# Opening of a one-core trunk kernel: key weights by a second queue, later loads behind the memory's splits, x's tiles later among the weight folds

## The chip, the cores and the metric

The kernel runs on one core of a Trainium2 chip. The time is that of the whole program on that core, in microseconds of the device, measured from outside; a profiled execution gives in addition a trace of every instruction. PE is the matmul engine, DVE the vector engine, ACT the scalar (activation) engine, POOL the general one, SP the engine that mostly issues DMAs. ACT can issue DMAs too, on a queue of its own. Each engine runs its instructions in the order in which they stand in its own stream, and waits for others by semaphores.

## The reference

A decoder layer of width 1024 over 2048 tokens: retention and a pooling mixer, then cross-attention into 256 memory tokens, then a gated MLP with a short convolution, each behind an RMSNorm and with a residual. Only this part matters here:

```python
def cross_attn(h, mem_n, wq, wkv, wo):
    q = (h @ wq).reshape(B, S, XA_HEADS, XA_HEAD_DIM)
    k, v = jnp.split(mem_n @ wkv, 2, axis=-1)
    ...
    s = jnp.einsum('bshd,bmhd->bhsm', q, k).astype(jnp.float32) * (XA_HEAD_DIM ** -0.5)
    p = jax.nn.softmax(s, axis=-1).astype(v.dtype)
    o = jnp.einsum('bhsm,bmhd->bshd', p, v).reshape(B, S, D_MODEL)
    return o @ wo
```

`mem_n` is the memory behind its RMSNorm. Keys and values depend on the memory and the weights alone, so the kernel folds `wq` into the keys and `wo` into the values once, ahead of the tokens. The layer's first step on the tokens, `rmsnorm(x, mix_norm_g)`, is also begun in that time.

## The kernel before

**Numbers.** Every float32 operand of a matmul is split into a high and a low part (`split`, L260 on): ACT writes the high part, DVE the low part (the source minus the high part), and `passes` (L276 to L278) makes three matmuls of each product: high by high, high by low, low by high. A weight tile of 128 x 1024 (512 KB) thus needs a load, one ACT and one DVE instruction before PE can use it.

**The opening** is `folded_weights` (from L428), a generator that a loop at L2087 runs item by item. The items, by number, are: keys K0 to K7 (items 0 to 7), values V0 and V1 (8, 9), then score folds M, values V, output folds O and pool folds W mixed:

```
0-7 K0..K7   8 V0   9 V1   10 M0   11 V2   12 M1   13 V3   14 M2   15 V4   16 M3
17 O0   18 V5   19 O1   20 V6   21 O2   22 V7   23 W0   24 W1   25 O3   26 W2   27 W3
```

- K*n* (`keys`, `project`) multiplies weight tile `wkv[n]` with the memory: 8 x 3 matmuls of 128 x 256. I write w0 to w15 for the tiles `wkv[0]` to `wkv[15]`; w8 to w15 are those of the values V0 to V7 (`memory_values`). With K2 the memory's norm is begun (`memory_norm`, L488): two squares on ACT, sums on DVE, and small matmuls (L357) with a column of the constants. With K7 the norm is spread over the keys (`spread`, L382) and the keys are scaled by it on DVE and split (`scaled_keys`, `parted`).
- M*h* (`score_weights`) needs the scaled and split keys of head *h* and two tiles of `wqT`: 48 matmuls of 128 x 256. Its results go to DRAM (`Md`) by ACT's queue.
- O*h* (`output_weights`) needs the values and two tiles of `wo`; W (`pool_weights`) one tile of `wout_p`.

**Places.** Loaded tiles stand in nine raw places of 512 KB: R0 to R2, S0, S1, Z0 to Z3 (L2084). A list gives out the place that was given back first. A weight's place is given back at once in program order (`new_raw`), so the next load into it waits only for the two splits of the tile before. An x tile (`load_x_wide`, L648) takes a place, is loaded by SP, split into `X` by ACT and DVE, squared in place by ACT and added to a running total by DVE; only then can its place be loaded again. The total stands in R0. The split parts of a weight stand in five wide places, used in turn.

In the order of before the list gives: w0 S0, w1 S1, w2 to w5 Z0 to Z3, w6 S0, w7 S1, x1 Z0, w8 R1, x2 R2, w9 Z1, x3 Z2, then M0's two tiles Z3 and S0, V2's weights S1, x4 Z0, M1's two tiles R1 and R2. R1 and R2 hold the memory at first.

**Order.** A planner orders each engine's stream by times of its own: among the instructions that it takes to be ready it places the one that stands first in the program, so that a load whose place is free can be moved ahead of loads that wait. `tc.keep_in_program_order` ties an instruction behind the one traced just before it on the same engine, and no more; `tc.issue_after` ties a block's instructions behind a named one. All four steps on an x tile, its load, and the splits of the memory and of w0 are tied in this way.

**Loads at the start.** L451 loads the memory in four parts of 256 KB, L453 the two halves of w0 (256 KB each) between them, L454 w1, all on SP; ACT issues the load of `vecs` (112 KB). L525 loads the constants (335.5 KB) with K1. Other sizes: `poolT` 256 KB and the positions twice 128 KB, whose calls stand with M3 and behind the folds. ACT's first work is its table load and one small activation (L455), then the splits in this order: memory 0, w0's first half, memory 1 to 3, w0's second half, memory 4 to 7. PE runs 9 small matmuls on a constant tile meanwhile (L458).

The x tiles come behind the items that L2086 names: x0 behind item 5, x1 behind 7, x2 behind 8, x3 behind 9, x4 behind 11, x5 behind 13, x6 behind 16, x7 behind 18. Behind item 21 the total goes through small matmuls (`rows_norm`, L2008), whose result is needed when the first values of the retention are evicted.

Of the kernel before, what the change touches and what calls it, by code (L numbers as in the profile page):

```python
# [22 lines left out]
SUB = 512  # L23
# [119 lines left out]
def trunk(ctx, tc, xT, memT, pos, w_qkgu, w_v, wkv, wqT, wo, wout_r, wout_p, poolT, w_up, w_dn, vecs, consts, outT):  # L143
# [136 lines left out]
    def new_raw():  # L280
        r = raws.take()
        r.free()
        return r.f
# [61 lines left out]
    def load_tile(src, room=None):  # L345
        raw = new_raw() if room is None else room.f
        fetched[0] = sp.dma_start(raw, src.rearrange("p k n -> p (k n)"))
        return raw
# [82 lines left out]
    def folded_weights():  # L431
# [17 lines left out]
        for q in range(4):  # L449
            to = memory[q // 2].f[:, q % 2 * SUB : (q % 2 + 1) * SUB].rearrange("p (k m) -> p k m", m=NMEM)  # L450
            sp.dma_start(to, memT.rearrange("(k p) m -> p k m", p=P)[:, 2 * q : 2 * q + 2])  # L451
            if q < 2:
                sp.dma_start(first[:, q * SUB : (q + 1) * SUB], wkv[0][:, 4 * q : 4 * q + 4].rearrange("p k n -> p (k n)"))  # L453
        second = load_tile(wkv[1])  # L454
        tc.keep_in_program_order(act.activation(warm.f[:, P : 2 * P], warm.f[:, :P], AF.Identity))  # L455
        lead = mmps()
        for _ in range(9):
# [8 lines left out]
        def wide_pair(raw, parts=1):  # L466
            u, w = wide(), T // parts
            for i in range(parts):
                split(raw[:, i * w : (i + 1) * w], *(r[:, i * w : (i + 1) * w] for r in u))
            return u  # L470
# [6 lines left out]
        u0 = wide()  # L477
        for k in range(KT):
            h, j = divmod(k, 4)
            split(memory[h].f[:, j * NMEM : (j + 1) * NMEM], mh[:, k], ml[:, k], memg[:, k : k + 1], kept="both")  # L480
            if k in (0, 3):
                at = slice(k // 3 * SUB, (k // 3 + 1) * SUB)
                split(first[:, at], u0[0][:, at], u0[1][:, at], kept="both")
        rm = TT.take()
        rn = smp.tile([P, 4], F32, tag="rnm", name="rnm", bufs=1)[:, :2]
        bank, done = [], []
# [11 lines left out]

        def project(n):

            u = u0 if n == 0 else wide_pair(second, 2) if n == 1 else wide_pair(load_tile(wkv[n]))
            if n % 2 == 0:
                bank[:] = [mmps()]
            at = n % 2 * NMEM
            ps = bank[0][:, at : at + NMEM]
            for k in range(KT):
                passes(ps, [r[:, k * P : (k + 1) * P] for r in u], (mh[:, k], ml[:, k]), k == 0, k == KT - 1)
# [13 lines left out]
        def keys(n):  # L521

            project(n)
            if n == 1:
                sp.dma_start(cs_t, consts)  # L525
            elif n == 2:
                memory_norm()
            if n % 2:
                done.append((n, bank[0]))
            if n == KT - 1:  # L530
                spread(rn, [rm.f[:, :NMEM]], late=True, behind=latest[0].ins)
                for pair in done:
                    scaled_keys(*pair)
                rm.free()
# [1548 lines left out]
    under[0], spacing[0] = weight_sums(), 2  # L2083
    raws = Places([(R, j * T) for j in range(3)] + [(r, 0) for r in S] + [(Z.arenas[0].t, j * T) for j in range(4)], T)  # L2084
    results = Places([(Z.arenas[1].t, j * T) for j in range(4)], T)
    wv, total, x_at = [], raws.take(), (5, 7, 8, 9, 11, 13, 16, 18)  # L2086
    for n, _ in enumerate(folded_weights()):  # L2087
        if n in x_at:
            load_x_wide(x_at.index(n), total)
        if n == 21:  # L2090
            total.back = None
            rn = rows_norm([total])
        if n in (24, 25):
            wv.append(value_weights(len(wv), 0))
        if n == 27:
            wv += [value_weights(kp, kp - 1) for kp in (2, 3)]
# [354 lines left out]
```

## Time and profile before

| | us |
|---|---|
| median of 3 runs | 2389.47 (2388.07 to 2391.1) |
| the profiled execution's own time | 2389.53 |
| its span in the trace | 2387.8 |
| PE busy | 2368.7 |
| DVE busy | 1796.6 |
| ACT busy | 1385.8 |
| POOL busy | 337.9 |

The span runs from the first to the last instruction of the trace; the time outside it is start and end of the launch. "Busy" is the time in which an engine runs at least one instruction. PE's matmuls overlap in the trace, so a busy PE can still run at a lower clock; the granted clock stands beside the busy times where stretches are listed. In a row of a timeline, "idle before" in square brackets is the time for which the engine stood still ahead of the instruction, with what ended it. The time to landing of a DMA runs from its issue to the semaphore that tells its end. The opening takes the first 116 us or so.

### The profile page before, as it was taken

What the parts mean: (1) busy time and instruction counts of PE and PEld (TensorE: products, weight loads), DVE (VectorE), ACT (ScalarE), POOL (GpSimd) and SP (SyncE); (2) the same over time, 40 slices, a digit from 0 to 9 for tenths busy, and PEclk for the clock granted to TensorE, in tenths of its full rate; (3) what the DMA queues carried; (4) which work ended last, traced back from release to release, by engine and by line L of the source; (5) the groups of instructions that cost most, each with busy time, mean ns of one, the idle gap of its engine ahead of it and who ended that gap; (6) DMA issues with size and microseconds to landing.
All of it is one profiled execution on the core that took longest, in us unless ns stands there. A gap on an engine that the chain in (4) does not pass through costs nothing.

```text
span 2387.8 us, 33436 instructions
## 1 busy us (share of the span) xinstructions
PE 2368.7 (99%) x11136; PEld 1980.8 (83%) x11136; DVE 1796.6 (75%) x2977; ACT 1385.8 (58%) x2507; POOL 337.9 (14%) x524
## 2 busy tenths in 40 slices
PE   8999999999999999999999999999999999999998
PEld 8888888888888888888888888888888888888886
DVE  8687876885767677866788776977677698877876
ACT  7845554663545545545655555855555577676663
POOL 0056554453041000000000010110000000000000
PEclk9999999999999999999999999999999999999999
DMA  8999999999594235486577564765455489768951
GB/s 308 343 285 294 280 264 285 284 308 310 164 260 123 79 119 159 151 281 228 170 238 251 179 199 135 243 207 176 150 177 188 136 261 316 234 183 284 343 174 73
DMA packets 269453, 527.78 MB, mean 221 GB/s; under 512 B 30048, under 2 KB 50912, under 8 KB 269280
## 3 DMA queue, kind: packets, MB, share of 16 engines
q1 hardware_dynamic: 212176, 402.83, 51.5%
q0 software_dynamic: 40960, 94.40, 16.5%
q10 hardware_dynamic: 16144, 28.43, 3.2%
q8 instruction: 87, 1.43, 0.2%
q14 instruction: 86, 0.70, 0.1%
HBM read 423.30 MB, written 196.61 MB: 260 GB/s over the span
## 4 chain that ended last, share of the span: by engine, by line
PE 97%; DMA 1%; DVE 1%; ACT 0%; issue 0%; SPq 0%; DVEq 0%; ACTq 0%
PE mm L276 30%; PE mm L278 30%; PE mm L277 30%; PE aux L276 1%; PE aux L278 1%; PE aux L277 1%; PE aux L800 1%; PE aux L774 1%; PE aux L785 1%; PE aux L947 1%; PE aux L802 1%; PE aux L357 0%; DMA S<-w_v 0%; DVE Z L248 0%; DMA Xd<-E 0%; PE aux L776 0%
## 5 line engine op out<-in xcount | busy, mean ns | idle before, releaser
L276 PE MATMUL mm<-G,Q 128*128 128x512 f32 (+1 forms) x1445 | 558.4, 388 | 4.3 <-DVE G L248 2.6
L277 PE MATMUL mm<-G,Q 128*128 128x512 f32 (+1 forms) x1445 | 558.7, 387 | 0.2 <-DVE G L256 0.2
L278 PE MATMUL mm<-G,Q 128*128 128x512 f32 (+1 forms) x1445 | 555.8, 387 | 0.2 <-DVE Q L248 0.2
L277 PE MATMUL mm<-G,E 128*128 128x512 f32 (+1 forms) x1072 | 409.4, 382 | 0.0
L276 PE MATMUL mm<-G,E 128*128 128x512 f32 (+1 forms) x1072 | 408.3, 382 | 0.3 <-DVE Z L248 0.3
L278 PE MATMUL mm<-G,E 128*128 128x512 f32 (+1 forms) x1072 | 408.0, 382 | 0.2 <-DVE E L248 0.2
L276 PEld LDWEIGHTS mm<-G,Q 128*128 128x128 f32 x1445 | 271.4, 188 | 60.2 <-issue 2.7
L277 PEld LDWEIGHTS mm<-G,Q 128*128 128x128 f32 x1445 | 271.5, 188 | 54.4 <-DVE G L248 0.4
L278 PEld LDWEIGHTS mm<-G,Q 128*128 128x128 f32 x1445 | 271.5, 188 | 54.4 <-DVE Q L248 0.4
L256 DVE SCALAR_TENSOR_TENSOR Z<-Z,vecs,Z 128x1024 f32<-128x1024 f32 x176 | 224.6, 1280 | 50.6 <-ACT Z L1219 47.0
L248 DVE TENSOR_TENSOR Z<-Z,mm 128x512 f32<-128x512 f32 (+1 forms) x290 | 193.5, 672 | 90.8 <-PE mm L278 88.8
L278 PEld LDWEIGHTS mm<-G,E 128*128 128x128 f32 x1072 | 201.5, 188 | 39.7 <-DVE E L248 0.6
L276 PEld LDWEIGHTS mm<-G,E 128*128 128x128 f32 x1072 | 201.4, 188 | 39.7 <-DVE Z L248 0.8
L277 PEld LDWEIGHTS mm<-G,E 128*128 128x128 f32 x1072 | 201.5, 188 | 38.9
L248 DVE TENSOR_TENSOR Q<-R,Q 128x512 fp32r<-128x512 f32 (+2 forms) x205 | 139.9, 683 | 84.3 <-ACT Q L1156 48.0
L248 DVE TENSOR_TENSOR T<-T 128x512 f32<-128x512 f32 (+4 forms) x196 | 133.9, 689 | 27.2 <-ACT T L424 13.3
L1156 ACT ACTIVATE Q<-R 128x512 fp32r<-128x512 f32 (+1 forms) x123 | 75.7, 617 | 133.0 <-PE mm L277 126.3
L1156 ACT ACTIVATE E<-R 128x512 fp32r<-128x512 f32 (+1 forms) x163 | 100.3, 615 | 71.0 <-PE mm L277 56.7
L1219 ACT ACTIVATE Z<-Z,vecs 128x1024 f32<-128x1024 f32 x88 | 109.1, 1241 | 32.3 <-DVE Z L248 31.3
L1103 ACT ACTIVATE G<-T 128x512 fp32r<-128x512 f32 x180 | 108.3, 623 | 32.4 <-DMA T<-Gd 22.4
L1156 ACT ACTIVATE Q<-S 128x512 fp32r<-128x512 f32 (+1 forms) x81 | 49.9, 616 | 98.6 <-PE mm L277 95.7
L248 DVE TENSOR_TENSOR Q<-S,Q 128x512 fp32r<-128x512 f32 (+1 forms) x112 | 75.9, 678 | 38.8 <-ACT Q L1156 30.1
(425 smaller groups left out, 4430.8 us busy)
## 6 DMA issues: line engine op xcount, KB each, us to landing
T<-Gd SPq DMA_DIRECT2D x168, 256.0 KB, 4.3
Ud<-w_up POOLq DMA_DIRECT2D x132, 256.0 KB, 9.7
Gd<-Z SPq DMA_DIRECT2D x110, 256.0 KB, 2.6
R<-Ud SPq DMA_DIRECT2D x104, 256.0 KB, 2.7
R<-w_up SPq DMA_DIRECT2D x82, 256.0 KB, 2.9
S<-Ud SPq DMA_DIRECT2D x72, 256.0 KB, 2.8
Gd<-T SPq DMA_DIRECT2D x56, 256.0 KB, 3.3
T<-Xd SPq DMA_DIRECT2D x53, 256.0 KB, 4.1
```

Source lines behind the costliest of these rows:

```text
L248: return eng.tensor_tensor(out=out, in0=a, in1=b, op=op)
L256: return dve.scalar_tensor_tensor(out=out, in0=a, scalar=s, in1=b, op0=op0, op1=op1)
L276: pe.matmul(ps, lh, rh, start=start, stop=False, skip_group_check=more)
L277: pe.matmul(ps, lh, rl, start=False, stop=False, skip_group_check=more)
L278: latest[0] = pe.matmul(ps, ll, rh, start=False, stop=stop, skip_group_check=more)
L774: pe.matmul(col(sc, c), self.ch(k, c), self.ch(q, c), start=True, stop=True)
L785: pe.matmul(col(kv, c), col(self.kn.f, c), self.ch(v, c, h * T), start=True, stop=True)
L800: pe.matmul(col(y, c), col(self.pr.f, c), self.ch(v, c, h * T), start=True, stop=self.cur[c] is None)
L802: pe.matmul(col(y, c), self.ch(q, c), self.cur[c], start=False, stop=True)
L1103: one = act.activation(hi, x, AF.Copy, scale=-1.0 if i == 2 else 1.0)
L1156: act.activation(p2[:, 0, :w], self.raw[i].f[:, :w], AF.Copy)
L1219: act.activation(self.c[g].f, a[:, 2:], AF.Identity, bias=cb[:, f : f + 1], scale=cw[2][:, f : f + 1])
```

## The change

Four edits in the opening.

1. The two halves of w0 are issued by ACT instead of SP.
2. w2 and w3 are loaded by ACT, through a new helper `load_early`, behind the memory's splits 3 and 7; K2 and K3 take those tiles instead of loading their own. The constants are loaded by ACT as well, behind the last split of the memory, instead of by SP with K1. All three are tied behind the instruction before them on ACT.
3. The list of free places is turned until S0 stands first. Without it w4 would get Z2. With it the list gives: w0 S0, w1 S1, w2 Z0, w3 Z1, w4 S0, w5 S1, w6 Z0, w7 Z1, w8 Z2, w9 Z3, x1 R1, M0's tiles R2 and S0, V2's weights S1, x2 Z0, M1's tiles Z1 and Z2, V3's weights Z3, x3 R1, M2's R2 and S0, V4's weights S1, x4 Z0, M3's Z1 and Z2, x5 Z3, O0's R1 and R2, V5's S0, x6 S1, O1's Z0 and Z1, V6's Z2, x7 Z3, O2's R1 and R2, V7's S0, the first pool fold's S1.
4. The x tiles come behind items 5, 9, 11, 13, 15, 16, 18 and 20, and the small matmuls of the total behind item 22.

```diff
             if q < 2:
-                sp.dma_start(first[:, q * SUB : (q + 1) * SUB], wkv[0][:, 4 * q : 4 * q + 4].rearrange("p k n -> p (k n)"))
-        second = load_tile(wkv[1])
+                act.dma_start(first[:, q * SUB : (q + 1) * SUB], wkv[0][:, 4 * q : 4 * q + 4].rearrange("p k n -> p (k n)"))
+        early = {1: load_tile(wkv[1])}
+
+        def load_early(n):
+            early[n] = new_raw()
+            tc.keep_in_program_order(act.dma_start(early[n], wkv[n].rearrange("p k n -> p (k n)")))
+
...
             if k in (0, 3):
                 at = slice(k // 3 * SUB, (k // 3 + 1) * SUB)
                 split(first[:, at], u0[0][:, at], u0[1][:, at], kept="both")
+            if k in (3, 7):
+                load_early(2 + k // 7)
+        tc.keep_in_program_order(act.dma_start(cs_t, consts))
+        while raws.one[raws.freed[0]].t is not S[0]:
+            raws.freed.append(raws.freed.pop(0))
...
-            u = u0 if n == 0 else wide_pair(second, 2) if n == 1 else wide_pair(load_tile(wkv[n]))
+            u = u0 if n == 0 else wide_pair(early.pop(n) if n in early else load_tile(wkv[n]), 2 if n == 1 else 1)
...
             project(n)
-            if n == 1:
-                sp.dma_start(cs_t, consts)
-            elif n == 2:
+            if n == 2:
                 memory_norm()
...
-    wv, total, x_at = [], raws.take(), (5, 7, 8, 9, 11, 13, 16, 18)
+    wv, total, x_at = [], raws.take(), (5, 9, 11, 13, 15, 16, 18, 20)
     for n, _ in enumerate(folded_weights()):
         if n in x_at:
             load_x_wide(x_at.index(n), total)
-        if n == 21:
+        if n == 22:
             total.back = None
             rn = rows_norm([total])
```

## Prediction

> **What bounds the kernel now.** I read the page first: how busy each engine is, and where the chain that ended last ran.
>
> ```profile
> span 2387.8 us, 33436 instructions
> ...
> PE 2368.7 (99%) x11136; PEld 1980.8 (83%) x11136; DVE 1796.6 (75%) x2977; ACT 1385.8 (58%) x2507; POOL 337.9 (14%) x524
> ...
> PE 97%; DMA 1%; DVE 1%; ACT 0%; issue 0%; SPq 0%; DVEq 0%; ACTq 0%
> ```
>
> The matmuls bound it, and the change takes none away. It can win only time in which PE stands still or runs at a lower clock: 2387.8 − 2368.7 = 19.1 us of standing still in all. The view of busy time by stretch (columns: length, then busy us of PE, PEld, DVE, ACT, POOL, granted clock, share of DMA time, GB/s) tells where that lies.
>
> ```profile
> 0.00:100.00 100.00, 92.42 (x660) 87.77 (x660) 71.81 (x95) 74.39 (x100) 0.20 (x4) 0.98 0.92 328
> ...
> 2375.00:2388.00 13.00, 3.55 (x20) 2.73 (x20) 6.43 (x18) 1.26 (x4) 0.00 (x0) 0.61 0.54 202
> ```
>
> 7.6 us of it lie in the first 100 us, the folding of the attention's weights that the change touches; the 9.5 us of the last stretch are the tail, which it does not touch. So I cut the first stretch finer and asked who PE waited for there (columns: total us, times, longest us).
>
> ```profile
> 37.60:40.40 2.80, 0.24 (x3) 0.06 (x2) 2.80 (x4) 2.80 (x6) 0.00 (x0) 1.00 0.33 63
> 40.40:53.30 12.90, 12.89 (x107) 12.90 (x108) 12.68 (x13) 8.85 (x11) 0.00 (x0) 1.00 0.74 235
> 53.30:56.40 3.10, 0.32 (x4) 0.12 (x2) 1.34 (x2) 2.29 (x3) 0.00 (x0) 1.00 1.04 418
> 56.40:60.20 3.80, 3.80 (x19) 3.80 (x20) 3.80 (x4) 2.77 (x4) 0.00 (x0) 0.55 1.03 404
> ```
>
> ```profile
> PE mm L276 <- ACT G L264: 3.0, 2, 2.8
> PE mm L276 <- DVE G L248: 2.6, 1, 2.6
> ```
>
> There are two holes: one of 2.6 us at 37.7, where the values (V0, V1) are done and the first score fold M0 waits for the scaled keys, and one of 2.8 us at 53.4, where the second score fold M1 waits for a weight. The second has a sequel: for 3.8 us behind it the granted clock is 0.55. There 19 matmuls take 3.80 us, where in the stretch ahead of it 107 take 12.89, or 0.120 each: 19 × 0.120 = 2.3, so the low clock costs another 1.5 us. All else in the first 100 us is 2 us in the first ten and crumbs.
>
> **Why M1 waits.** The chain of waits and the timelines of SP, DVE and ACT give it (columns: start, us, engine, line, operation, what ended the idle time before).
>
> ```profile
> 23.88 0.42 SPq L652 DMA_DIRECT2D R<-xT  x1
> ...
> 48.60 0.33 SPq L474 DMA_DIRECT2D R<-wqT  x1
> ```
>
> ```profile
> 47.34 1.23 DVE L248 TENSOR_TENSOR R<-R 128x1024 f32<-128x1024 f32 x1
> ```
>
> ```profile
> 55.25 1.06 ACT L264 ACTIVATE G<-R 128x1024 fp32r<-128x1024 f32 x1 [0.33 <-DMA R<-wqT]
> ```
>
> M1's second tile of wqT gets raw place R2, which x2 has held since 23.88. x2 leaves it only with its sum of squares (47.34 to 48.57), since the sums go in order and x1's comes first. The load starts at 48.60, lands 6.6 us later, and is split from 55.25 to 56.31, and then PE goes on.
>
> **Third part of the change, the x tiles.** They now come behind items 5, 9, 11, 13, 15, 16, 18, 20. Following the list of places with the new order gives M1's two tiles Z1 and Z2, which key 7's and value 0's weights leave once split, by 30 us; no x is ahead. The hole at 53.4 and its low clock go: 2.8 + 1.5 = **4.3 us**. Nothing is taken away, as all eight x tiles keep their two ACT and two DVE instructions, some 4.7 us in a row:
>
> ```profile
> 60.21 1.14 ACT L267 ACTIVATE G<-Z,vecs 128x1024 fp32r<-128x1024 f32 x1
> 61.39 1.28 DVE L256 SCALAR_TENSOR_TENSOR G<-Z,vecs,G 128x1024 fp32r<-128x1024 f32 x1 [0.95 <-ACT G L267]
> 63.63 1.07 ACT L654 ACTIVATE Z<-Z 128x1024 f32<-128x1024 f32 x1
> 64.74 1.22 DVE L248 TENSOR_TENSOR R<-R,Z 128x1024 f32<-128x1024 f32 x1 [0.21 <-ACT Z L654]
> ```
>
> The two more that now fall behind 58 us cost ACT 2 × 2.2 and DVE 2 × 2.5 us. These stretches can hold them:
>
> ```profile
> 60.20:80.00 19.80, 19.80 (x154) 19.23 (x153) 12.52 (x11) 15.79 (x22) 0.00 (x0) 1.00 0.99 345
> 80.00:98.00 18.00, 18.00 (x105) 15.89 (x104) 9.06 (x8) 13.77 (x19) 0.00 (x0) 1.00 1.01 364
> ```
>
> ACT has 4.0 and 4.2 us free, DVE 7 and 9. What is late next is again a place: by the new list the first tile of the first output fold O0 gets R1, where x3 stands, and x3 is kept behind V3's last split. From M0's start, M0, V2, M1 and V3 are 144 matmuls of 0.120, so V3 ends 17.3 us behind it (57.4, with the 40.1 found below); x3's four steps end at 62.1. A tile of wo lands 5.7 to 8.2 us after its issue:
>
> ```profile
> S<-wo SPq DMA_DIRECT2D x1, 512.0 KB, 5.7
> ```
>
> ```profile
> Z<-wo SPq DMA_DIRECT2D x1, 512.0 KB, 8.2
> ```
>
> That is 67.8 to 70.3, and 2.3 more for its two splits 70.1 to 72.6, where O0 starts at 57.4 + 14.4 = 71.8. I charge **0.5 us** (0 to 1.5, as x3 may queue behind M2's evictions). The norm's small matmuls only change places with V7; their count stays.
>
> **Second part, the later keys' weights.** w2 and w3 (keys 2 and 3) and the constants leave SP's queue for ACT's, behind w0's second split and behind the eighth split of the memory. The constants are first needed by the norm at 23 us, so they cost nothing. w2 matters:
>
> ```profile
> 6.99 0.63 ACT L264 ACTIVATE Q<-S 128x512 fp32r<-128x512 f32 x1 [0.40 <-DMA S<-wkv]
> ...
> 11.73 1.06 ACT L264 ACTIVATE E<-Z 128x1024 fp32r<-128x1024 f32 x1 [0.96 <-DMA Z<-wkv]
> ```
>
> ```profile
> 14.11 0.39 PE L278 MATMUL mm<-G,E 128*128 128x256 f32 x1
> ```
>
> Now w2 is issued at 4.71, lands at 11.7 and key 2's first low matmul runs at 14.11, 2.4 us behind the landing, with ACT waiting 0.96 us for it: there is no slack. In the new order the issue cannot come before 7.1, just behind the split that starts at 6.99. And SP, relieved, does not stand still. The planner pulls a load forward once its place is free:
>
> ```profile
> 9.62 0.38 SPq L594 DMA_DIRECT2D T<-poolT  x1
> ...
> 13.06 0.33 SPq L347 DMA_DIRECT2D S<-wkv  x1
> ```
>
> poolT and pos belong far behind key 7, whose load at 13.06 they pass. By the new list V0's and V1's weights (w8, w9) get the unused Z2 and Z3, so I expect them, poolT and pos right behind w1, ahead of w2. That is memory 1024 + w0 512 + vecs 112 + w1 512 + w8, w9 1024 + poolT 256 + pos 256 = 3696 KB. What has moved by then is in the DMA view of the first 60 us (slices of 1.5 us):
>
> ```profile
> GB/s 0 163 375 334 370 389 412 415 423 412 420 330 244 346 382 401 410 410 401 421 388 298 322 287 19 0 137 314 243 5 130 274 341 270 216 407 416 421 419 385
> ```
>
> ```profile
> Z<-wkv SPq DMA_DIRECT2D x1, 512.0 KB, 7.0
> ```
>
> By 7.1: 1.5 × (163 + 375 + 334) + 1.1 × 370 = 1715 KB, so 1981 KB stand ahead of w2, 2493 with it. The w2 of now had 2130 KB with it (3007 issued, 877 moved) and took 7.0 us. Upper end, one line for both queues: 7.0 × 2493 / 2130 = 8.2 us, landing at 15.3. Lower end, ACT's queue gets half: 1024 KB at 410 GB/s, 2.5 us, and the 1.8 us by which the 7.0 exceed 2130 KB at that rate, so 4.3 us, landing at 11.4. No load on ACT's queue beside a busy SP queue is in the trace; the nearest rows are its stores, which land no sooner than SP's loads beside them:
>
> ```profile
> Md<-Z ACTq DMA_DIRECT2D x1, 512.0 KB, 6.8
> R<-wo SPq DMA_DIRECT2D x1, 512.0 KB, 6.2
> ```
>
> So I take 7.0 us: landing at 14.1, and key 2 **2.4 us** later than now (0 to 3.6). w3, asked for 2 us behind w2, is then needed 2.9 us behind it and costs nothing more.
>
> The Trainium skill, page "DMA: Bandwidth & Descriptors", section "Queues, rings and completion order", says that each DMA engine takes turns between the queue rows that have work, packet by packet. By that w2 has its half, the lower end, and the sum below would be 6.2 instead of 4.1; the store that took 6.8 beside 6.2 speaks against it, though not for loads.
>
> What the delay costs is read at M0, the next meeting point. Now:
>
> ```profile
> 31.69 0.40 PE L382 MATMUL aux<-Q,ones 128*128 128x256 f32 x2
> ...
> 37.56 0.28 PE L278 MATMUL mm<-G 128*128 128x256 f32 x1
> 40.41 0.35 PE L276 MATMUL mm<-G,Q 128*128 128x256 f32 x1 [2.57 <-DVE G L248]
> ```
>
> ```profile
> 33.71 1.29 DVE L256 SCALAR_TENSOR_TENSOR G<-R,vecs,G 128x1024 fp32r<-128x1024 f32 x1 [0.35 <-ACT G L267]
> ...
> 37.31 2.35 DVE L248 TENSOR_TENSOR E<-S,E 128x1024 fp32r<-128x1024 f32 x2
> 39.58 2.48 DVE L248 TENSOR_TENSOR G<-mm,G 128x512 fp32r<-128x512 f32 x4
> ```
>
> From the norm's spread at 31.69 to the first low key at 40.3 pass 8.6 us, with x2's split (33.71) and two late weight splits (37.31) between. x2 goes, and M0's second tile, whose place S0 is free earlier, should be split ahead: 8.6 − 1.2 − 1.2 = 6.2. Starting 2.4 later the keys are ready at 34.1 + 6.2 = 40.3 at most, V1's matmuls end at 37.68 + 2.4 = 40.1. So M0 starts at about 40.1 where it started at 40.41: the hole fills, but with the delay of w2, and only **0.3 us** are won (2.4 if w2 is on time, since the keys then end near 38.0; −0.9 at the upper end of w2).
>
> **First part, w0 by ACT's queue.** I take 0 (−0.4 to +0.5). The issues take as long, and the DMA engines are full (370 GB/s from 6 to 7.5 us). Two more issues, some 0.5 us each, ahead of ACT's table load move its end from 2.5 to 3.5:
>
> ```profile
> 1.21 1.28 ACT L455 ACT_TABLE_LOAD   x1 [1.21 <-PEq L2443]
> ...
> 4.15 0.51 ACT L267 ACTIVATE G<-R,vecs 128x256 fp32r<-128x256 f32 x1 [1.34 <-DMA R<-memT]
> ```
>
> ACT's wait for the memory's first tile (1.34, to 4.15) hides that and would still be 0.3 us; without that cover the first split would come 1 us later. If w0's second half lands sooner, key 0 ends sooner, and what is late next is w1's landing, then w2's.
>
> **The sum:** 4.3 + 0.3 − 0.5 + 0 = 4.1 us. The profiled execution takes 2389.53 us, 1.7 more than its span and 0.06 above the median; 2389.5 − 4.1 = **2385.4**. About 0.2% (4.8 us) is what a measurement of this kernel can tell from no change, so this lies just within.
>
> **Rivals.**
> - w2 is on time, because ACT's queue gets its half or w8 and w9 are not pulled ahead. For it: ACT's queue is empty then; against it: its stores beside SP's loads. Then 4.3 + 2.4 − 0.5 = 6.2: 2383.3. Chance 0.30.
> - The x tiles go and PE still waits: the order is a planner's, made with times of its own, and as many weights stand behind an x as before. One miss the size of the second hole takes its 4.3 back, for about 2389.5. Against it: only O0's first tile is near its due time. Chance 0.13.
> - Slower: the same holding of places along the whole row. O0's first tile stands behind x3 (R1), O1's behind x4 (Z0), the first pool weights behind x6 (S1), and the sums go in order, so one late x makes all later ones late; SP's queue, which waits in order, passes it on to the loads behind. Each miss costs a hole and a low clock, 4.3, once a tile lands 2.8 us too late: x3's sum at about 65 instead of 62. Two misses (8.6) already eat the 4.6 won, three make 12.9 − 4.6 = 8.3 lost: 2397.8. For it: O0's margin is near nothing. Against it: O1 comes 8 us behind O0, and x4 needs neither V3 nor a load behind x3's. Chance 0.07.
>
> **How the numbers follow.** My forecast has 0.50, of which 0.08 reach past 4.8 us, since w2 can be anywhere between its ends. Faster by over 0.2%: 0.30 + 0.08 = 0.38; within: 0.42 + 0.13 = 0.55; slower: 0.07. The range goes from 2381.5 (w2 on time, no charge at O0, and the start's half us and a little more) to 2389.5 (one hole remains).
>
> **What would show it.** M1 starting without a wait, no stretch at a clock of 0.55 behind it: third part right. w8 and w9 on SP before 6 us and w2's split on ACT beginning at about 14: second part right; a split at 11 to 12 is the first rival. M0's start near 40: the hole filled by delay. A wait of PE on a wo tile near 72: the charge at O0. The forecast fails if PE stands still behind 100 us where it did not before, as the planner may reorder anything behind the change.

## The result, and the profile after

| | before | after |
|---|---|---|
| median, us | 2388.77 (2386.8 to 2391.1, 6 runs) | 2404.41 (2402.91 to 2408.1, 6 runs) |
| ratio | | 1.0068, 95% interval 1.0055 to 1.0081 |
| span of the profiled execution | 2387.8 | 2401.1 |
| PE idle in it (span less busy) | 19.1 | 27.6 |

The medians lie 15.6 us apart, and the ratio says 0.68%: the change costs time. The forecast was a gain of 4.1 us. The page of the kernel after, by its first lines:

```profile
span 2401.1 us, 33430 instructions
PE 2373.5 (99%) x11136; PEld 1982.6 (83%) x11136; DVE 1796.3 (75%) x2977; ACT 1386.4 (58%) x2507; POOL 337.0 (14%) x524
...
PE 95%; DMA 2%; DVE 1%; ACT 1%; issue 0%; SPq 0%; DVEq 0%
```

PE stands still for 8.5 us more and is busy for 4.8 us longer with as many matmuls: some of them ran at a low clock. In the chain that ended last, DMA's share went from 1% to 2%. The view by stretch, of after (columns as in the prediction):

```profile
0.00:100.00 100.00, 85.97 (x604) 82.01 (x605) 65.59 (x90) 67.27 (x89) 0.20 (x4) 0.97 0.83 287
40.00:50.00 10.00, 4.60 (x29) 4.22 (x29) 10.00 (x15) 7.45 (x12) 0.00 (x0) 0.88 0.56 163
80.00:90.00 10.00, 7.16 (x40) 6.38 (x39) 4.81 (x4) 4.25 (x6) 0.00 (x0) 0.83 1.04 409
```

In the first 100 us PE starts 604 matmuls; before it was 660. The last two columns matter as much: the DMA engines moved 287 GB/s in that time, before 328. Whom PE waited for in the first 130 us (total, times, longest):

```profile
PE mm L276 <- ACT G L264: 4.1, 1, 4.1
PE mm L278 <- DVE E L248: 3.3, 2, 3.1
PE mm L276 <- ACT E L264: 2.2, 2, 1.8
PE mm L276 <- ACT Q L264: 2.1, 2, 1.1
PE mm L277 <- DVE G L248: 1.3, 1, 1.3
```

The first 100 us hold three places of more than 1 us behind the start; a fourth wait, of 1.35 us, comes at 120.5. **K2** (18.5 us, 3.07): w2's load was issued at 7.38 and its split began at 13.27, but on DVE the scaling of the pool factors, whose load SP had pulled forward, stood ahead of w2's low part and waited for its own landing. The timeline of DVE:

```profile
16.64 0.69 DVE L248 TENSOR_TENSOR T<-T,vecs 128x512 f32<-128x512 f32 x1 [3.77 <-DMA T<-poolT]
17.25 1.22 DVE L248 TENSOR_TENSOR E<-Z,E 128x1024 fp32r<-128x1024 f32 x1
```

**M0** (46.3 us, 4.05 and 1.35, and a low clock behind it). DVE again:

```profile
39.02 1.28 DVE L256 SCALAR_TENSOR_TENSOR G<-Z,vecs,G 128x1024 fp32r<-128x1024 f32 x1
40.22 1.22 DVE L248 TENSOR_TENSOR G<-Z,G 128x1024 fp32r<-128x1024 f32 x1
41.35 0.68 DVE L248 TENSOR_TENSOR Q<-T,Q 128x512 fp32r<-128x512 f32 x1
41.96 2.48 DVE L248 TENSOR_TENSOR mm<-mm,T 128x512 f32<-128x512 f32 x4
44.35 1.21 DVE L248 TENSOR_TENSOR G<-Z,G 128x1024 fp32r<-128x1024 f32 x1
45.48 0.68 DVE L248 TENSOR_TENSOR G<-mm,G 128x512 fp32r<-128x512 f32 x1
46.09 1.27 DVE L256 SCALAR_TENSOR_TENSOR G<-R,vecs,G 128x1024 fp32r<-128x1024 f32 x1
47.28 1.28 DVE L248 TENSOR_TENSOR G<-mm,G 128x512 fp32r<-128x512 f32 x2
```

The scaled keys are ready at 44.4, but the low parts of the keys (47.28) come behind x2's split (39.02), M1's two weight splits (40.22, 44.35), a split of V1's values (45.48) and x1's split (46.09). **O0** (82.1 and 84.4 us, 1.03 and 1.81, and a low clock): x3's sum ended at 77.3, and only then could the load into R1 go out. DVE, ACT and PE:

```profile
76.05 1.23 DVE L248 TENSOR_TENSOR R<-R 128x1024 f32<-128x1024 f32 x1 [0.21 <-ACT R L662]
```
```profile
83.33 1.06 ACT L264 ACTIVATE E<-R 128x1024 fp32r<-128x1024 f32 x1 [0.77 <-DMA R<-wo]
```
```profile
84.44 1.57 PE L276 MATMUL mm<-E,G 128*128 128x512 f32 x4 [1.81 <-ACT E L264]
```

M1 no longer waits. Compared by the start of the same matmul, counted from the first, PE is behind the kernel before by 4.4 us at 20 us, 8.8 at 50, 4.4 at 60 (the old second hole is gone), 9.3 at 100, 11.1 at 120, 10.9 at 500 and 13.1 at 700.

### The profile page after: what moved, and what is told of

It reads as the page before. It is cut to its first block, busy times and chain, and to the rows that moved or that the text cites. A ratio compares the mean times of both kernels' runs of the same rounds, so it can differ in the third digit from the quotient of the medians.

```text
span 2401.1 us, 33430 instructions
## 1 busy us (share of the span) xinstructions
PE 2373.5 (99%) x11136; PEld 1982.6 (83%) x11136; DVE 1796.3 (75%) x2977; ACT 1386.4 (58%) x2507; POOL 337.0 (14%) x524
## 4 chain that ended last, share of the span: by engine, by line
PE 95%; DMA 2%; DVE 1%; ACT 1%; issue 0%; SPq 0%; DVEq 0%
PE mm L276 30%; PE mm L278 30%; PE mm L277 30%; PE aux L276 1%; PE aux L278 1%; PE aux L277 1%; DMA S<-w_v 1%; PE aux L808 1%; PE aux L782 1%; PE aux L793 1%; PE aux L955 1%; PE aux L810 1%; DMA T<-poolT 0%; PE aux L357 0%; DVE Z L248 0%; DMA R<-w_v 0%
## 5 line engine op out<-in xcount | busy, mean ns | idle before, releaser
L276 PEld LDWEIGHTS mm<-G,E 128*128 128x128 f32 x1072 | 201.8, 188 | 40.1 <-DVE Z L248 0.8
L248 DVE TENSOR_TENSOR T<-T 128x512 f32<-128x512 f32 (+4 forms) x196 | 133.7, 688 | 26.9 <-ACT T L424 12.9
L1164 ACT ACTIVATE E<-R 128x512 fp32r<-128x512 f32 (+1 forms) x163 | 100.3, 615 | 69.2 <-PE mm L277 54.1
L248 DVE TENSOR_TENSOR Q<-S,Q 128x512 fp32r<-128x512 f32 (+2 forms) x115 | 79.4, 691 | 37.1 <-ACT Q L1164 29.9
L248 DVE TENSOR_TENSOR E<-aux,E 128x512 fp32r<-128x512 f32 (+1 forms) x136 | 88.9, 656 | 21.3 <-ACT E L1164 16.5
```

The costliest lines, as they stand in the source:

```text
L248: return eng.tensor_tensor(out=out, in0=a, in1=b, op=op)
L276: pe.matmul(ps, lh, rh, start=start, stop=False, skip_group_check=more)
L1164: act.activation(p2[:, 0, :w], self.raw[i].f[:, :w], AF.Copy)
```

## The experiments

All ratios are to the kernel before, measured beside each run. "PE late" is how much later than in the profile of before the same matmul starts, by count, at 100, 500 and 700 us of the latter; "MB" is what all DMA engines had moved by 590 us; "left" is what POOL's queue still moved from 590 to 615 us (both explained below). One launch of a kernel differs from the next by several us (29 of before: 2386.0 to 2394.5), and "PE late" is that of one launch: those profiled of g1, g4 and h3 lay 3.0, 2.9 and 4.4 us above their medians. For g3 its 42 additional matmuls are not counted.

| run | ratio, 95% interval | PE late, us | MB | left |
|---|---|---|---|---|
| before | | | 175.1 | 0.03 |
| after | 1.0068 (1.0055 to 1.0081) | 9.3, 10.9, 13.1 | 171.0 | 2.7 |
| e1_w0_act_only | 1.0001 (0.9992 to 1.0011) | −1.8, −1.9, −1.9 | 175.5 | 0.0 |
| e2_x_moved_only | 1.0046 (1.0032 to 1.0061) | 6.1, 11.2, 13.3 | 172.0 | 1.5 |
| e3_start_only | 1.0045 (1.0030 to 1.0060) | 3.2, 10.7, 10.4 | 172.3 | 1.5 |
| e4_pool_held | 1.0063 (1.0048 to 1.0078) | 10.4, 11.6, 18.1 | 170.0 | 3.5 |
| f1_held | 1.0056 (1.0041 to 1.0070) | 11.1, 12.7, 16.8 | 170.4 | 3.1 |
| f2_keys_first | 1.0044 (1.0026 to 1.0061) | 4.9, 8.0, 12.5 | 171.2 | 3.0 |
| f3_output_turn | 1.0057 (1.0042 to 1.0072) | 7.8, 12.2, 14.4 | 170.6 | 3.0 |
| f4_all_three | 1.0035 (1.0022 to 1.0048) | 0.4, 4.8, 8.5 | 172.9 | 1.9 |
| g1_before_swap | 1.0019 (1.0011 to 1.0028) | −0.8, 0.4, 6.8 | 173.5 | 1.4 |
| g2_before_swap_keys | 1.0035 (1.0022 to 1.0047) | 2.6, 3.7, 7.2 | 173.2 | 1.5 |
| g3_before_delay | 1.0048 (1.0035 to 1.0061) | 3.0, 4.1, 10.0 | 172.1 | 2.8 |
| g4_before_late_copy | 1.0017 (1.0006 to 1.0028) | −0.7, 0.5, 6.7 | 175.3 | 1.6 |
| h1_sums_later | 1.0009 (1.0000 to 1.0018) | −1.2, −0.1, 4.0 | 170.8 | 0.03 |
| h2_sums_ahead | 1.0011 (1.0002 to 1.0019) | −2.4, −0.7, −0.8 | 175.0 | 0.2 |
| h3_swap_sums_ahead | 1.0030 (1.0020 to 1.0040) | −0.6, 3.3, 10.6 | 172.4 | 2.4 |
| h4_three_sums_ahead | 1.0071 (1.0058 to 1.0084) | 0.8, 14.9, 16.7 | 170.1 | 3.4 |
| i1_swap_turn | 1.0026 (1.0017 to 1.0036) | −0.6, 8.5, 9.2 | 172.7 | 1.6 |
| i2_three_turn | 1.0045 (1.0031 to 1.0060) | 0.9, 5.3, 10.5 | 172.3 | 2.4 |

### The parts of the change alone

**e1**, on before: only the two halves of w0 by ACT's queue. **e2**, on before: only x's items and the norm's place. **e3**, on after: x's items as before. **e4**, on after: the pool table's load behind w6's.

```diff
e1 -                sp.dma_start(first[:, q * SUB : ...
e1 +                act.dma_start(first[:, q * SUB : ...
e4 +            with tc.issue_after(sixth[0].ins):
                     sp.dma_start(r3, poolT.rearrange("g p c -> p g c"))
```

> The kernel of before with the first part alone: w0's two halves are issued by ACT, all else stays on SP. Theory A (the loss of 15.6 us is made in three places: key 2's low half held behind the pool factors' scaling on DVE, the scaled keys held behind more splits on DVE, the first output fold behind x3's place; the first part adds under 1 us): within 1.5 us of before; key 0 starts about 0.9 us later than at 5.44, as in the changed kernel, and w1's landing takes most of it back. Theory B (the second queue itself upsets the start): 3 us or more slower.

> The kernel of before with the third part alone: the x tiles behind items 5, 9, 11, 13, 15, 16, 18, 20 and the total's norm behind item 22. The list of places then gives O0's first tile R2, where x3 stands. Theory A: the hole ahead of M1 goes, but M0 starts no earlier than 40.4 and O0 waits 2 to 3 us for its first tile with a low clock behind it: 0 to +6 us against before. Theory C (all of the loss comes from the x tiles): +12 us or more. Theory D (all of it from the loads at the start, and the x tiles bring what was predicted): -3 to -5 us.

> The changed kernel with the x tiles and the norm behind the old items (5, 7, 8, 9, 11, 13, 16, 18; 21): parts one and two alone. Theory A: key 2's low half again runs behind the scaling of the pool factors at about 17.2 and its first low matmul at 18.5; M0 starts 2 to 6 us later than at 40.4; +3 to +9 us against before. Theory C: within 1.5 us of before. Theory D: +15 us or more.

> The changed kernel with one edit: the load of the pool factors is tied behind key 6's load on SP, so that the planner puts their scaling on DVE behind key 5's split and not ahead of key 2's. Theory A: the wait of 3.8 us on DVE and PE's wait of 3.1 us in key 2 shrink to what w2's landing leaves (DVE free at once when ACT has split w2 at 14.3, first low matmul at about 15.6 instead of 18.5): K1 to V1 end 2.5 to 3 us earlier, and the whole is 2 to 4 us faster than the changed kernel, that is +11 to +13.5 against before. If the wait was w2's own landing (rival): no faster than the changed kernel.

The queue of w0 is worth nothing. Each of the other halves costs two thirds of the whole, 11 us of 2389 each, so they do not add up. Both hit M0: it waits 3.59 us in e2 and 4.08 us in e3. In e4 the pool factors no longer stand in w2's way, but there w2 itself took 7.7 us to its split (issue at 8.28, split at 15.95) and nothing was won.

### The three holes, mended one by one in the kernel after

**f1**: w8, w9, the pool's table and the positions behind w6's load. **f2**: x1, x2 and M1's two tiles behind the keys' splits (their loads too). **f3**: the list turned so that O0's first tile does not get R1. **f4**: all three.

```diff
f1 +            with tc.issue_after(sixth[0].ins) if n in (KT, KT + 1) else nullcontext():
f2 +            with behind_keys() if n in x_at[1:3] else nullcontext():
                     load_x_wide(x_at.index(n), total)
f3 +            if h == 0:
f3 +                raws.freed.insert(3, raws.freed.pop(0))
```

> The changed kernel, with the loads that the second queue's program order pulled forward on SP (w8, w9, the pool's table, the positions) held behind w6's load, so that SP's order is again mem, w1, w4, w5, x0, w6 and so on. Theory (w2 came late because SP's own loads were in flight beside it and because the pool factors' scaling stood ahead of its split on DVE): w2 lands by about 12 instead of 13.2, PE reaches K2's first low part at about 14.5 instead of 18.5, the time falls by 2 to 4 us against the kernel after. Rival (the chain of the keys sets M0 whatever K2 does): M0 starts at the same time as in the kernel after, its hole is longer by what K2's is shorter, and the time stays within 1 us.

> The changed kernel, with x1's and x2's splits and M1's two weight splits held behind the keys' last split on ACT and on DVE. Theory (the places that the change frees let these splits go ahead of the keys' on DVE, and that is M0's hole of 4.05 and 1.35 us and the low clock behind it): M0 starts 3 to 4 us earlier, its second wait goes, no low clock behind it; M1 may wait up to 2 us for its second tile. The time falls by 3 to 6 us against the kernel after. Rival (the keys' chain is set by the spread and the statistics ahead of it, not by DVE's queue): M0's wait stays at 4 us or more, and the time within 1 us.

> The changed kernel, with the list of places turned by one ahead of the first output weight, so that its two tiles take a place held by values' weights and the next after it, not the place that x3 holds until its sum at about 77 us. Theory (O0's first tile waits for x3's sum): its load goes out some 10 us earlier, the waits of 1.03 and 1.81 us at 82 to 85 us and the low clock behind them go, and the time falls by 3.5 to 4.5 us. Rival (the second tile, or DVE's order, binds there too): a wait of 1 us or more is left at O0, and the time falls by less than 2 us.

> The changed kernel with the three edits of the other runs of this set together (loads held, keys' splits first, places turned). Theory (the three holes are three causes and add up): 9 to 14 us faster than the kernel after, so 2390 to 2395 us, near the kernel before. Rival (what the opening gains is given back where the DMA engines are full, at 400 to 620 us, since the loads there set the end): PE is ahead of the kernel after by 8 us or more at 200 us but by less than 5 us at 700 us, and the time is above 2399.

Two of the edits take their holes away, the third a part. In f1 K2 has no wait; M0's then is 6.04, as the rival said. In f3 PE waits for nothing from 70 to 100 us. In f2 M0's waits go from 4.05 and 1.35 to 1.79, but the low clock behind them stays (0.57 from 46 to 50 us), and M0 starts only 0.6 us earlier; in f4 M0 still waits 3.71, so DVE's order is not its whole cause (the section on why the prediction was wrong has the rest). Alone the edits bring little: of the 0.68% of the kernel after, f1 and f3 leave 0.56% and 0.57% and f2 0.44%, with intervals that overlap that of after. And f4, which is only 0.4 us late at 100 us, still ends 0.35% behind: 4.5 us are lost at 100 to 120 us (ACT's order and a late store) and 3.7 between 500 and 700 us. That late loss was unexplained, and it is what the remaining runs are about.

### The old holes, mended without moving x

**g1**, on before: M1's second tile gets Z1, V3's weights x2's place R2. **g2**: also x2's and V2's splits behind the keys'. **g3**, on before: 42 more matmuls behind M1. **g4**, on before: four more copies of 512 KB, DRAM to DRAM, at 120 to 170 us.

```diff
g1 +            if h == 1:
g1 +                raws.freed[1:3] = raws.freed[2], raws.freed[1]
g3 +                    for _ in range(42):
g3 +                        pe.matmul(more_ps[:, :NMEM], ones, mh[:, 0], start=True, stop=True)
g4 +            tc.keep_in_program_order(act.dma_start(spare[t0 // 2], wqT[t0 * P : (t0 + 1) * P, :]))
```

> The kernel before, with the second and third places of the list exchanged ahead of M1, so that M1's second tile takes the place that w9 left and V3's weights the place of x2. Nothing else is moved. Theory (the second hole is one place, and can be had without moving x): M1 starts without its wait of 2.8 us and without the low clock behind it, PE is 4 us ahead of the kernel before at 60 us; V3 may wait up to 1 us for its tile. If PE alone bounds the time behind 100 us, the end is 3.5 to 4.5 us earlier. Rival (behind 120 us the DMA engines are the bound, and PE's lead is lost to waits for loads there): the lead at 100 us is 4 us, the end within 1.5 us of the kernel before.

> The kernel of the run g1_before_swap, with x2's two splits and those of V2's weights tied behind the keys' splits on ACT and on DVE; their loads are left free. Theory (the first hole is the two DVE instructions between the scaling and the keys' low parts): M0 starts at about 38 instead of 40.4, PE is 6 to 6.5 us ahead of the kernel before at 60 us, and the end is 5.5 to 6.5 us earlier. Rival (DMA engines the bound behind 120 us): no more than 1.5 us are left at the end. Other rival (V2's weights are late now): a wait of 1 us or more at 43 to 47 us.

> The kernel before with 42 more matmuls of 128 x 256 behind M1's last one (their result is not used): PE is held for 42 x 0.120 = 5.0 us at about 62 us, and neither the loads' order nor x's place is changed. Theory (a delay of the opening grows behind 120 us, as DMA time not used there is not made up): the lag is 5 us at 100 us and 8 to 11 us at 700 us, as 7.4 grew to 14 in the run e2_x_moved_only and 4.6 to 10.5 in e3_start_only. Rival 1 (only the changed order of the loads makes the lag grow): 5 us at 100 us and 4.5 to 5.5 at the end. Rival 2 (PE has slack there): under 3 us at the end.

> The kernel before with four more copies of 512 KB from DRAM to DRAM (2 MB, used by nothing), issued on ACT's queue behind the four groups of evictions of the first values, so between 120 and 170 us; the opening is as before. Theory (from 120 to 600 us the DMA engines are the bound, at about 0.29 MB per us): the block sums on POOL's queue end 5 to 7 us later, and PE waits at 440 to 450 or 590 to 620 us for so much, so the time is 5 to 7 us longer. Rival (loads and sums have slack there, and it is the order that counts): under 1.5 us.

g1 is the sharpest run of the study. It takes away the second hole: PE is 4.0 us ahead at 60 us. Small waits (0.56 us at 57.5, 0.86 at 69.2 and others) leave 0.8 of it at 100 us. PE is level from 120 to 590 us and then, in the launch that was profiled, loses 6.6 us by 620, with waits that the kernel before does not have. PE of g1:

```profile
602.28 0.50 PE L276 MATMUL mm<-Z,Q 128*128 128x512 f32 x1 [2.53 <-ACT Q L264]
...
610.63 0.50 PE L276 MATMUL mm<-Z,Q 128*128 128x512 f32 x1 [0.82 <-ACT Q L264]
...
612.02 0.50 PE L278 MATMUL mm<-Z,Q 128*128 128x512 f32 x1 [0.66 <-DVE Q L248]
```

What PE waits for there is a weight that the opening itself wrote, VWd, read back by SP. The DMA view from 590 to 615 us, first before, then g1:

```profile
q0 software_dynamic: 25, 0.03, 0.7%
...
R<-VWd SPq DMA_DIRECT2D x1, 512.0 KB, 3.6
```
```profile
q0 software_dynamic: 872, 1.39, 33.0%
...
R<-VWd SPq DMA_DIRECT2D x1, 512.0 KB, 8.8
```

Queue q0 is POOL's. It carries the **block sums** (L1051 and L1054): from 120 to 740 us POOL adds blocks of weights in DRAM by accumulating DMAs, and each turn of them is released by a small copy on ACT (L1070), which the loop over the values calls step by step. In the kernel before the sums due by then are done at 590 us, and the load lands in 3.6 us. In g1 1.39 MB of them are left, 0.91 MB move while the load is out, and it takes 8.8. All 20 profiles agree: from its issue to its split the load took 3.4 to 3.8 us in the five where the sums moved 0.01 MB or less meanwhile (before, e1, e2, e3, h1), and 4.9 to 9.7 us in the fifteen where they moved 0.1 to 1.0 MB. Why the sums are late is read from the stretches, before and g1:

```profile
0.00:100.00 100.00, 92.42 (x660) 87.77 (x660) 71.81 (x95) 74.39 (x100) 0.20 (x4) 0.98 0.92 328
100.00:590.00 490.00, 488.42 (x2354) 407.59 (x2354) 371.22 (x729) 265.27 (x583) 240.77 (x373) 1.00 1.04 291
```
```profile
0.00:100.00 100.00, 93.23 (x666) 87.28 (x667) 71.42 (x96) 74.98 (x100) 0.20 (x4) 1.00 0.91 331
100.00:590.00 490.00, 488.00 (x2346) 406.63 (x2345) 371.07 (x727) 264.65 (x581) 238.07 (x370) 1.00 1.04 286
```

From 100 to 590 us the DMA engines have no free time: a share of 1.02 to 1.05, and 281 to 291 GB/s, in every run of this study. What is not moved there in time is mostly not made up (h2 is the exception: 2.0 MB behind at 400 us, 0.2 at 590, with a wait of 1.53 us between). g1 lost it at 120 to 135 us, where the third turn came 6 us later (POOL, before and g1):

```profile
128.27 0.30 POOL L1071 COPY halo<-halo 128x2 f32<-128x2 f32 x1 [1.70 <-ACT halo L1070]
```
```profile
134.31 0.33 POOL L1073 COPY halo<-halo 128x2 f32<-128x2 f32 x1 [7.37 <-ACT halo L1072]
```

ACT's copy stands behind the same split in both; in g1 that split waited 5.70 us for DVE, and why DVE stood still is not shown. The kernel after loses it in the opening instead: 287 GB/s up to 100 us, 4.1 MB less than before, and then 290, so that at 590 us it still lacks 4.1 MB. At 0.29 MB per us that is 14 us; PE is 13.1 late at 700 us. The table's column "MB" can be read in this way throughout: what a run lacks of 175.1, over 0.29, is PE's lateness at 700 us within 2 us in 17 of 19 kernels (e1 −1.4 for −1.9, e4 17.6 for 18.1, f4 7.6 for 8.5; g4, with its own 2.1 MB taken off, 6.6 for 6.7). The others are e2 (10.7 for 13.3) and h1 (14.8 for 4.0). In part this holds of itself, since a late PE asks for its loads late: after was 9.3 us late at 100 us already, by its holes. What speaks for DMA as the cause is the order of events in g1 and e3, which lack bytes first and lose PE's time later, and g4: there nothing is changed ahead of 120 us, 2 MB are added, and 0.17% is lost. g3 agrees: PE is held for 5.0 us, the second hole takes part of it, 3 us are left at 100 us and 10.0 at 700.

g2 shows the same together with a hole of 5.25 us at 70.7 us ahead of M3, whose last tile was issued only at 61.09, behind the sum of the x tile in its place, and split on ACT at 69.56: the first hole is gone, and its 2.6 us did not reach the end.

### Can the sums be moved?

**h1**, on before: no turn of the sums in the first two steps. **h2**, on before, **h3**, on g1: the turn ahead of the quarter sums in each step. **h4**: f4 with x's and M1's loads left free, and the turn ahead. **i1**, **i2**: g1 and f4 with two turns at the second step and none at the tenth.

```diff
h1 -            if b == 0:
h1 +            if b == 0 and place[0] > 2:
                     next(under[0], None)
i1 +            for _ in range({2: 2, 10: 0}.get(place[0], 1) if b == 0 else 0):
                     next(under[0], None)
```

> The kernel before, with the block sums' turns left out of the first two steps of the values' loop, so that the first turn comes some 8 us later (at about 128 instead of 119 us); the opening is untouched. Theory (the block sums run behind PE from 120 to 740 us and PE's loads at 590 to 620 us share the DMA engines with them; a late start of the sums is paid there): PE is level with the kernel before up to 500 us, and stands 5 to 9 us longer between 590 and 620 us; the time is 5 to 9 us longer. Rival (the order of loads in the opening makes the late holes): no change beyond 1.5 us.

> The kernel before, with the sums' turn ahead of the quarter sums in each step of the values' loop, so that each turn on ACT stands one step earlier (the first at about 115 instead of 119 us). Theory: the hole of 0.41 us at 589 us goes, nothing else is to be had there, 0 to 1 us faster. Rival (earlier sums take DMA time from the first values' loads): a wait behind 105 us, up to 2 us slower.

> The kernel of the run g1_before_swap (M1's second tile not in x2's place) with the sums' turn ahead of the quarter sums. Theory: the third turn comes by 129 instead of 134 us, the waits of 2.53, 0.82 and 0.66 us at 600 to 612 us go, 5 to 7 us are won against g1_before_swap, which puts it 0 to 2 us ahead of the kernel before. Rival (the late holes have another cause): within 2 us of g1_before_swap, 4 us behind the kernel before.

> The changed kernel with the three edits of f4_all_three, but with only the splits of x1, x2 and M1 tied behind the keys' and their loads left free, and with the sums' turn ahead of the quarter sums. Theory: PE is 1 to 2 us ahead of the kernel before at 60 to 90 us as in f4_all_three, the sums start by 120 us, and the late holes shrink from 3 us to under 1: 2388 to 2394 us. Rival (ACT's stand of 5.4 us for a store at 93 to 98 us, or another order of the stores, stays): PE 4 us behind at 120 us, the time 2395 or more.

> The kernel of the run g1_before_swap with two turns of the block sums at the second step of the values' loop (about 124 us) and none at the tenth. Theory (the sums' lag of 1.1 MB at 200 us makes the waits at 590 to 615 us): the sums' queue has moved 13.5 MB or more by 200 us, less than 0.7 MB of it is left behind 590 us, PE's waits at 600 to 612 us fall from 4.0 to under 1.5 us, and the time is 3 to 5 us below g1_before_swap, so level with the kernel before (2387 to 2391 us). Rival (the DMA engines are full from 120 us on, so sums that come earlier only push the loads back): as much is left behind 590 us as in g1_before_swap, within 1.5 us of its time.

> The kernel of the run f4_all_three with the same two turns at the second step and none at the tenth. Theory: less than 1 MB of the sums is left behind 590 us instead of 1.86, the waits there fall from 3.0 to under 1.5 us, and the time is 2 to 3 us below f4_all_three (2396 to 2398 us). Rival: within 1 us of f4_all_three.

h1 leaves the opening as it was and loses 5.2 us of PE's time between 400 and 700 us in its profile (waits of 0.99, 1.91 and 0.75 us), but only 0.09% in the ratio: less than expected. Its turns are moved by a step, so that fewer sums were due by 590 us, and it is the run that the column "MB" misjudges most. My stronger theory, that a start of the sums in time takes the late waits away, has one test, i1, and **fell** there. h3, h4 and i2 do not test it, since their edits did not bring the sums forward: by 200 us the queue had moved 10.7, 10.3 and 10.8 MB, less than in g1 and f4 (12.9 and 11.9). In i1 the sums' queue had moved 13.8 MB by 200 us (before 14.0, g1 12.9), as expected, and the waits at 600 us fell from 4.0 to 0.7, but PE stood still elsewhere:

```profile
171.92 0.50 PE L276 MATMUL mm<-G,Q 128*128 128x512 f32 x1 [1.67 <-ACT E L1791]
```
```profile
447.38 0.79 PE L276 MATMUL mm<-G 128*128 128x512 f32 x1 [2.89 <-ACT G L267]
```
```profile
445.57 0.63 ACT L264 ACTIVATE G<-R 128x512 fp32r<-128x512 f32 x1 [3.76 <-DMA R<-Md]
```

The wait at 447 us is that of a load: the last row is ACT, just ahead of it. This agrees with the rival of i1, that with the engines full, sums that come earlier push the loads back, and as much was left behind 590 us as in g1 (1.6 MB and 1.4). The wait at 172 us is for an eviction on ACT, and no load stands right ahead of it. No version beat the kernel before. What stays open is how many of the 15.6 us belong to DMA alone, since each edit also lets the planner put ACT's and PE's streams in another order, and why f4's and i2's ACT waits for a store at about 100 us.

## Why the prediction was wrong

The forecast had PE 4.1 us ahead behind O0. In the profile of after it was 9.3 us behind at 100 us: 4.4 lost at K2 (2.4 in the sum), another 4.4 at M0 (where the sum had the hole filled and 0.3 won), 4.4 won at M1 (4.3), and 4.9 lost at O0 (0.5). Another 3.8 us went between 100 and 700 us, for which the sum had no term.

**The second hole, 4.3 us: the mechanism right, the size a single sample.** M1 lost its wait. But five profiles of this study have the opening of the kernel before, untouched (before, g3, g4, h1, h2), and there M1 waits 2.78, 1.04, 2.23, 0.93 and not at all:

```profile
55.60 0.39 PE L276 MATMUL mm<-G 128*128 128x256 f32 x1 [1.04 <-ACT G L264]
```
```profile
55.57 0.39 PE L277 MATMUL mm<-G 128*128 128x256 f32 x1 [2.23 <-ACT G L265]
```
```profile
56.33 0.39 PE L276 MATMUL mm<-G 128*128 128x256 f32 x1 [0.93 <-ACT G L264]
```
```profile
52.00:60.00 8.00, 8.00 (x67) 7.82 (x66) 7.07 (x7) 6.24 (x8) 0.00 (x0) 1.00 1.00 375
```

The last row is h2: PE is busy from 52 to 60 us at full clock. The mean wait is 1.4 us, and a low clock followed in two of the five. In the other three the low clock stood behind M0's wait instead, which is 2.6 us in all five:

```profile
39.58:42.99 3.41, 2.88 (x13) 2.91 (x14) 3.41 (x6) 2.37 (x3) 0.00 (x0) 0.50 0.72 280
```

That is g3; h1 and h2 have the same, before and g4 not. There PE came to M1 1.3 to 1.5 us later and found its weight nearly or quite ready. So the hole and its low clock were no fixed price of M1, and the largest term of the sum was the largest value of five.

**M0, 0.3 us: the step that failed first** was "ready at 34.1 + 6.2": the norm's spread 2.4 us later than before, at 34.1, and from there "8.6 − 1.2 − 1.2 = 6.2" to the first low key, at 40.3. In the kernel after the spread came at 39.23 and the first low key at 47.96, 8.7 us behind it. So 5.1 of the 7.7 us were lost ahead of the spread and 2.5 behind it. Ahead of it K2 was late by 4.4 instead of 2.4, and the planner had put the spread 26 matmuls later into PE's stream (26 × 0.120 = 3.1 us), which the sum never asked about. PE's row of the spread, and PE's matmuls up to it, after and before:

```profile
39.23 0.28 PE L382 MATMUL aux<-Q,ones 128*128 128x256 f32 x1
```
```profile
0.00:39.23 39.23, 33.43 (x241) 32.31 (x241) 26.07 (x51) 23.72 (x31) 0.20 (x4) 1.00 0.92 328
```
```profile
0.00:31.69 31.69, 29.46 (x215) 28.08 (x215) 23.68 (x48) 20.52 (x27) 0.20 (x4) 1.00 0.97 355
```

g2 and f4 tell the two apart. Both put the keys' splits first on DVE; in g2 the spread stands where it stood before and M0's hole is gone, in f4 it stands 31 matmuls later and M0 waits 3.71 us. Why the planner moved the spread is not shown. Behind the spread it was DVE: I took x2's split and M0's second split out of the keys' way and did not ask what would come in. The early places (Z1, Z2 for M1) that I had found for the second hole let M1's splits, x1 and x2 go ahead of the keys on DVE: before, two splits stand between the scaling and the low parts; after, three, with two more ahead of the scaling; and V1's matmuls ended at 42.3 instead of the 40.1 of the sum. f2 shows DVE's part: with the keys' splits first, the first low key ends 4.7 us behind the spread (40.90 to 45.57).

**w2, 2.4 us: the load near, the term 4.4.** The load took 5.9 us (estimated 7.0) and its split began at 13.3 (14.1). The sum let SP pull the pool's table forward and left out the DVE instruction that it feeds. PE was 4.4 us late at 20 us. From issue to split w2 took 5.9 to 7.7 us in the five kernels in which SP had sent out w8 or w9 and the positions ahead of it (after, e3, e4, f2, f3), and 3.6 to 3.8 in the four that hold those behind w6 (f1, f4, h4, i2). The queues of the DMA view from 7.4 to 10.5 us, first after (SP's queue is the only one in it), then f1, where q10 is ACT's queue:

```profile
q1 hardware_dynamic: 350, 1.29, 103.8%
```
```profile
q10 hardware_dynamic: 84, 0.34, 44.8%
q1 hardware_dynamic: 130, 0.39, 30.8%
```

In after none of w2 moved in these 3 us, though it was issued at 7.38, and 1.29 MB of SP's loads did: w2 had no half of the engines but stood behind what SP had issued, as at the upper end of the sum. The Trainium skill, page "DMA: Bandwidth & Descriptors", section "Queues, rings and completion order", has each DMA engine take turns between the queue rows that have work; the estimate by it, half of the engines' time for w2, was 4.3 us. This stretch of after does not show such turns.

**O0, 0.5 us: the place named, the size wrong.** x3's sum ended at 77.3, not at 62, since M0 was late and x3's splits stood behind x4's and x5's on ACT (70.1 after 61.7 and 66.2) and on DVE. The third rival (places held by x along the row, chance 0.07) is in its first member what happened. Its two others did not come.

**w0, 0: right** (e1, 1.0001). The Trainium skill, page "DMA: Bandwidth & Descriptors", section "Issuing engines are not separate DMA queues", says that DMAs of all engines share the 16 and that issuing on several saves only issue time; e1 agrees.

**What the sum did not have at all** is the stretch behind 100 us, though the prediction named it as a sign of failing: PE waits at 120.5 us (1.35) and loses 2.4 us between 590 and 620. In f4, level at 100 us, 8.1 us go there; at such a loss even 4.1 us ahead at 100 us would not have been kept. I read where PE stands still and treated the rest as bound by PE. The view by stretch gives 1.04 for DMA from 100 to 590 us, and I had quoted 0.92 for the first 100. With that, moving x's eight tiles (4 MB) to later had a price that no wait of the kernel before shows: at 0.29 MB per us, every MB that the opening leaves for later costs, by my estimate, up to 3.4 us. g1, which has the third part's gain alone (4.0 us at 60 us) and is 0.19% slower, shows that this gain did not reach the end even where its step was right.

## What to carry to other kernels

Where a long stretch keeps the DMA engines full beside a busy PE, count bytes moved by a given time as well as PE's holes: an edit ahead of that stretch that closes a hole and delays loads can lose. When a buffer becomes free earlier, list what the scheduler will now put ahead of the critical instruction on each in-order engine, PE included, not only what leaves its way. And a hole of 2 to 3 us in one profile is one draw; take a second profile before its size becomes a term.

## What the runs showed of the hardware

- PE's clock was low behind waits of 2.78 us (before) and 2.23 us (g4: 0.57 from 56 to 60 us), and stayed at 1.00 behind one of 2.57 (before, M0), while behind the same wait of M0 it was 0.50 from 39.58 to 42.99 us in g3. The Trainium skill, page "TensorE: Matmul & The Clock Gate", section "What's actually happening", has the low state follow at least one idle window of about 3.4 us; here shorter waits had it too, and not each time. The low stretches of the openings last 3.41, 6.83 or 10.24 us in the clock records, so the clock is set in steps of 3.41 us. Ahead of the low stretches of before and g3 PE was busy for 0.63 and 1.38 us of such a step, and behind one with 1.63 the clock stayed full: M0's wait in before lay across two steps.

```profile
53.28:56.69 3.41, 0.63 (x5) 0.43 (x4) 1.63 (x2) 2.58 (x3) 0.00 (x0) 1.00 1.04 420
56.69:60.10 3.41, 3.41 (x18) 3.41 (x17) 3.41 (x4) 2.38 (x4) 0.00 (x0) 0.50 1.03 402
```
```profile
36.17:39.58 3.41, 1.38 (x12) 1.18 (x10) 3.41 (x5) 3.41 (x7) 0.00 (x0) 1.00 0.21 19
```
```profile
36.21:39.62 3.41, 1.63 (x14) 1.42 (x12) 3.41 (x5) 3.41 (x6) 0.00 (x0) 1.00 0.03 12
```

- In the full stretch the engines moved 281 to 291 GB/s with POOL's accumulating sums among the traffic, and 409 GB/s where only plain loads and stores ran (80 to 90 us of after), at about the same share (1.02 to 1.05, and 1.04).
- The same 512 KB load, VWd, landed in 3.6 us with POOL's queue empty (before) and in 8.8 with 0.91 MB of its sums moving meanwhile (g1).
- A 512 KB load issued on ACT's queue moved its first bytes 3.5 us after its issue while SP's queue had a backlog (after), and 1.0 us after it where SP's loads were held (f1).
